# Output projections with 512-column matmuls, one weight tile at a time over all token blocks

## The chip, the cores and the metric

One core of one Trainium2 chip runs the whole program. The metric is device time in microseconds (us) of one execution; the kernel before takes 1948.97 us, the median of 3 runs that lie between 1947.54 and 1953.53 us.

## What is computed

A two-layer encoder step over 2048 prompt tokens and 8 samples of 16 tokens, d_model 1024, all in float32. Layer 0 joins banded attention and a gated delta rule, layer 1 takes trailing means. Each layer ends in an output projection of 1024 x 1024 that is added to the residual; these two products are what the change touches:

```python
def ab_layer(h, ...):
    ...
    y = h + jnp.concatenate([o_a, o_b], axis=-1) @ w_out
def pool_layer(h, ...):
    ...
    y = h + (mixed * jax.nn.silu(gate)) @ w_out
```

## The kernel before

Tokens are taken in four groups (`GROUPS`): group 0 has four prompt blocks and the one sample block of 128 tokens (nb = 5), groups 1 to 3 have four prompt blocks (nb = 4). For each group the program runs layer 0 and then layer 1. To keep float32 accuracy every product is three matmuls: operand and weight are each split into a rounded part and a rest (hi, lo), and hi x hi, hi x lo and lo x hi are summed in one PSUM bank.

**Weights** stream through a ring of three tiles (`wp`, tag "w", `NWB` = 3), hi and lo together 1 MB. In group 0 a tile is loaded from the input in float32 (`w_load`, L447), split by ACT (cast, L459) and by POOL and DVE (subtract, L463; `SHARE` says which rows of it POOL takes), and stored to a scratch copy `wk` (`w_store`, L472). In groups 1 to 3 it is loaded from `wk` (L436). `weight()` for tile n issues the load of tile n + 2, which must wait until tile n - 1 is no longer read. All DMAs are issued by one engine, SP, in program order.

**The output projection** is `out_half` (L713 to L732). It is called twice per layer, each time for half of the 1024 contraction rows (`ops0`, `ops1`: four operands of 128 rows each), so eight times in all. A weight tile holds four row blocks by 256 columns. For every tile the blocks of tokens are taken in turn; each block gets 12 matmuls of 256 columns in one PSUM bank of the tag "pj" (two banks), and then VectorE (DVE) adds the result to the residual `y1[b]` (L729). Where `done` is given (second half of a layer), the last two tiles are taken together, block by block, and after each block `done(b)` is called: in layer 0 it normalises the finished row block for layer 1 (`normed`: L514 to L534, later transposes L543), in layer 1 it issues the store of the output row block (L1774).

```python
for k, (oh, ol) in enumerate(ops):
    mm(pp[:, 0:256], oh[:, tk], wh[:, k, :], start=(k == 0), stop=False)
    mm(pp[:, 0:256], oh[:, tk], wl[:, k, :], start=False, stop=False)
    mm(pp[:, 0:256], ol[:, tk], wh[:, k, :], start=False, stop=(k == 3))
```

**Side work** runs in generators that are advanced by `tick(us)`, called between matmuls: the program's order is set by this assumed time, and a scheduler then fixes the order on each engine. During `out_half` of layer 1 the input of the next group is prepared (`norm_input`): two chunks of two blocks; of each, x is loaded (L508) and squared (L514, L516), POOL forms the inverse root (`rs`, L489), TensorE (PE) transposes it (L577), and L583 to L586 write the operand XH, XL. After the last `out_half` of a group comes `tok_major` of the next one (L1255 to L1257), which uses two weight tiles, the first for k < 4 and the second for k >= 4. PSUM has eight banks: two each for the tags "pj", "rc", "sc" and "tp". "rc" and "sc" serve the attention and delta-rule jobs, which are finished before `out_half` starts.

Of the kernel before, what the change touches and what calls it, by code (L numbers as in the profile page):

```python
# [10 lines left out]
ALU = mybir.AluOpType  # L11
# [4 lines left out]
P = 128  # L16
# [74 lines left out]
def weight_plan():  # L91

    import numpy as np

    plan = []

    def add(part, cut):
        plan.append((part, cut))

    def cols(name, c):  # L100
        return lambda w: w[name][:, c].reshape(KT, P, len(c)).transpose(1, 0, 2)

    def rows(name, k0, c0):
        return lambda w: w[name].reshape(KT, P, D)[k0:k0 + 4, :, c0:c0 + 256].transpose(1, 0, 2)

    def k_half(name, k0, c):
        return lambda w: w[name].reshape(KT, P, -1)[k0:k0 + 4][:, :, c].transpose(1, 0, 2)

    def out_rows(pr, c0):
        def cut(w):  # L110
            a = w["out"][0:512].reshape(2, 4, 64, D)[:, 2 * pr:2 * pr + 2, :, c0:c0 + 256]
            b = w["out"][512:].reshape(4, P, D)[2 * pr:2 * pr + 2, :, c0:c0 + 256]
            return np.concatenate([a.transpose(0, 2, 1, 3).reshape(P, 2, 256), b.transpose(1, 0, 2)], axis=1)
        return cut

    def grp(gi):
        return lambda w: w["grp"][gi].reshape(2, P, 256).transpose(1, 0, 2)

    def span(c0, n):
        return np.arange(c0, c0 + n)  # L120

    def keys(pr):
        for h in (2 * pr, 2 * pr + 1):
            add("B", cols("in", span(C_B + 512 + P * h, P)))

    def queries(pr):
        for o in (0, 1024):
            for h in (2 * pr, 2 * pr + 1):
                add("B", cols("in", span(C_B + o + P * h, P)))

    def queries_a(pr):
        c = np.concatenate([span(C_Q + 256 * g + P * pr, P) for g in range(2)])
        for k in range(2):
            add("A", k_half("in", 4 * k, c))

    for k in range(2):
        add("A", k_half("in", 4 * k, np.concatenate([span(C_K, 256), span(C_BA, 8)])))
    for pr in range(2):
        keys(pr)
        if pr == 0:  # L140
            queries_a(pr)
        queries(pr)
        if pr:
            queries_a(pr)
    for pr in range(2):
        for h in (2 * pr, 2 * pr + 1):
            add("G", cols("in", span(C_BG + P * h, P)))
        for j in (2 * pr, 2 * pr + 1):
            add("G", cols("in", np.concatenate([span(C_G + 256 * g + 64 * j, 64) for g in range(2)])))
    for pr in range(2):  # L150
        for c in range(4):
            add("O", out_rows(pr, 256 * c))
    for gi in range(4):
        for o in (0, D):
            for i in (2 * gi, 2 * gi + 1):
                add("C", cols("in_c", span(o + P * i, P)))
        add("W", grp(gi))
    for hf in range(2):
        for c in range(4):
            add("O", rows("out_c", 4 * hf, 256 * c))  # L160
    return plan

W_SHAPE = {"B": (8, P), "G": (8, P), "C": (8, P), "O": (4, 256), "W": (2, 256), "A": (4, 256)}
W_FIRST = (4, 264)

VECS = [("g_ab", KT), ("g_c", KT), ("scale", KT), ("o_norm", 1), ("q_norm", 1), ("taps", 48), ("k_norm", 64), ("k_col", 1),
# [63 lines left out]
def hybrid_kernel(  # L232
# [241 lines left out]
    def weight():  # L474
        n = wpos[0]
        wpos[0] += 1
        while wpos[1] <= min(n + 2, len(plan) - 1):
            w_load(wpos[1])
            wpos[1] += 1
        w_split(n + 1)  # L480

        w_store(1)
        if n + 1 == nw:
            w_store(0)
        return ready.pop(n)
# [180 lines left out]
    def group(gix, norm_job):  # L666
# [43 lines left out]
            drop(a)  # L710
            return [(h[:, i, 0:n], lo[:, i, 0:n]) for i in range(2)], [h, lo]

        def out_half(ops, y1, done=None):  # L713

            steps = [(0,), (1,), (2,), (3,)] if done is None else [(0,), (1,), (2, 3)]
            for cs in steps:
                ws = [weight() for _ in cs]
                for b in range(nb):
                    tk = slice(P * b, P * b + P)
                    for c, (wh, wl) in zip(cs, ws):  # L720
                        pp = psum("pj")
                        for k, (oh, ol) in enumerate(ops):
                            mm(pp[:, 0:256], oh[:, tk], wh[:, k, :], start=(k == 0), stop=False)  # L723
                            mm(pp[:, 0:256], oh[:, tk], wl[:, k, :], start=False, stop=False)  # L724
                            mm(pp[:, 0:256], ol[:, tk], wh[:, k, :], start=False, stop=(k == 3))  # L725
                            if k == 1:
                                tick(0.64)
                        ysl = y1[b][:, 256 * c:256 * c + 256]
                        V.tensor_tensor(ysl, pp[:, 0:256], ysl, op=ALU.add)  # L729
                        if done is not None and c == 3:  # L730
                            done(b)
                        tick(0.64)  # L732

        finish(norm_job)

# [909 lines left out]

                queue.append(cols())

        out_half(ops1, y1, normed)
        drop(*used1)
        drain()  # L1650

# [119 lines left out]
        out_half(ops0, y1)  # L1771
        drop(*used0)
        drain()
        out_half(ops1, y1, lambda b: Q.dma_start(rows(y, b), y1[b]))  # L1774
        drop(*used1)
        drop(*y1)

# [25 lines left out]
```

## Time and profile before

| | |
|---|---|
| median of 3 runs | 1948.97 us |
| profiled execution, its own time | 1951.19 us |
| its span | 1949.2 us, 34495 instructions |
| PE busy / weight loads (PEld) / DVE / ACT / POOL | 96% / 87% / 63% / 39% / 25% |
| DMA engines | 48.8% of their span for the one queue, 172 GB/s |

The span is that of the profiled execution; its own time is 2 us longer. Matmuls overlap in the pipe, so the durations of single matmuls add up to more than their busy time: how fast a stream of them runs is read from the distance of their starts. PE is the engine that is nearly always busy; idle time of the others costs nothing unless PE waits for it.

### The profile page before, as it was taken

Reading aid. Unit: us, or ns where it says so; the run is one execution under the profiler, and the core shown is the slowest. Engines: PE = TensorE matmul, PEld = TensorE weight load, DVE = VectorE, ACT = ScalarE, POOL = GpSimd, SP = SyncE. Lnnn points to the kernel's source line nnn. Section 1 sums busy time; section 2 is a strip of 40 time slices with the busy share of each in tenths; the row PEclk is TensorE's granted clock in tenths of the full one; section 3 lists DMA queues with packets and bytes.
Section 4 is the critical chain, followed back from the end, with each engine's and each line's share of the span. In section 5 each row is a group of like instructions: output and inputs, shape, how many; then the busy total and the mean of one; then the engine's idle time right before and its main releaser. Section 6 shows DMA issues by size and latency. Waiting matters only on the chain.

```text
span 1949.2 us, 34495 instructions
## 1 busy us (share of the span) xinstructions
PE 1863.0 (96%) x12994; PEld 1687.7 (87%) x12994; DVE 1218.5 (63%) x3439; ACT 758.5 (39%) x1954; POOL 496.2 (25%) x628
## 2 busy tenths in 40 slices
PE   5988989999999999899999999999999999999999
PEld 4988888899999888789889888789889978789889
DVE  5797967545665597764445597764345597764442
ACT  5465336333332474442221474442221474342210
POOL 3622451423343413210112413210111413110000
PEclk8998999999999999999999999999999999999999
DMA  7343363655677533434467533434567533434454
GB/s 261 96 161 133 109 217 101 221 190 212 211 264 263 200 115 118 151 120 173 178 218 261 176 114 115 151 121 172 188 218 263 183 114 101 158 115 173 172 193 176
DMA packets 93875, 335.13 MB, mean 172 GB/s; under 512 B 35805, under 2 KB 44253, under 8 KB 64269
## 3 DMA queue, kind: packets, MB, share of 16 engines
q1 hardware_dynamic: 93708, 332.92, 48.8%
q8 instruction: 103, 1.69, 0.3%
q14 instruction: 64, 0.52, 0.1%
HBM read 254.31 MB, written 78.58 MB: 171 GB/s over the span
## 4 chain that ended last, share of the span: by engine, by line
PE 76%; DVE 14%; issue 3%; DMA 2%; POOL 2%; ACT 2%; SPq 0%; DVEq 0%; POOLq 0%; ACTq 0%
PE pj L688 12%; PE pj L690 12%; PE pj L689 12%; PE pj L723 6%; PE pj L724 6%; PE pj L725 6%; DVE tm L969 3%; DVE A L970 2%; PE pj L1255 1%; PE pj L1257 1%; PE pj L1256 1%; PE tp L1434 1%; PE rc L1140 1%; DVE B L846 1%; DMA w<-wk 1%
## 5 line engine op out<-in xcount | busy, mean ns | idle before, releaser
L688 PE MATMUL pj<-XH,w 128*128 128x512 f32 (+3 forms) x1488 | 543.5, 365 | 5.4 <-ACT cb L826 3.3
L689 PE MATMUL pj<-XL,w 128*128 128x512 f32 (+3 forms) x1488 | 535.5, 360 | 0.0
L690 PE MATMUL pj<-XH,w 128*128 128x512 f32 (+3 forms) x1488 | 534.7, 359 | 0.3 <-POOL w L463 0.3
L688 PEld LDWEIGHTS pj<-XH,w 128*128 128x128 f32 x1488 | 283.9, 191 | 34.6 <-ACT cb L826 3.5
L690 PEld LDWEIGHTS pj<-XH,w 128*128 128x128 f32 x1488 | 283.6, 191 | 30.9 <-POOL w L463 0.6
L689 PEld LDWEIGHTS pj<-XL,w 128*128 128x128 f32 x1488 | 284.2, 191 | 27.7 <-issue 0.7
L725 PE MATMUL pj<-w,B 128*128 128x256 f32 x864 | 243.5, 282 | 0.0
L723 PE MATMUL pj<-w,B 128*128 128x256 f32 x768 | 217.8, 284 | 1.4 <-DVE A L729 1.4
L724 PE MATMUL pj<-w,B 128*128 128x256 f32 x768 | 217.3, 283 | 1.5 <-POOL w L463 1.5
L725 PEld LDWEIGHTS pj<-w,B 128*128 128x128 f32 x864 | 164.3, 190 | 0.0
L463 POOL TENSOR_TENSOR w<-wst,w 128x640 fp32r<-128x640 f32 (+3 forms) x60 | 112.1, 1870 | 145.2 <-ACT w L459 136.3
L723 PEld LDWEIGHTS pj<-w,B 128*128 128x128 f32 x768 | 146.5, 191 | 1.9 <-DVE A L729 1.6
L724 PEld LDWEIGHTS pj<-w,B 128*128 128x128 f32 x768 | 145.5, 189 | 1.7 <-POOL w L463 1.7
L729 DVE TENSOR_TENSOR B<-pj,B 128x256 f32<-128x256 f32 x144 | 60.8, 422 | 100.4 <-PE pj L725 99.5
L1255 PE MATMUL pj<-w,XH 128*128 128x256 f32 (+1 forms) x368 | 108.7, 296 | 5.2 <-DMA w<-wk 4.8
L1257 PE MATMUL pj<-w,XL 128*128 128x256 f32 (+1 forms) x368 | 106.1, 289 | 0.0
L1256 PE MATMUL pj<-w,XH 128*128 128x256 f32 (+1 forms) x368 | 105.8, 288 | 0.0
L729 DVE TENSOR_TENSOR A<-pj,A 128x256 f32<-128x256 f32 x128 | 54.0, 422 | 79.6 <-PE pj L725 79.3
L723 PE MATMUL pj<-w,A 128*128 128x256 f32 x320 | 91.5, 286 | 0.0
L724 PE MATMUL pj<-w,A 128*128 128x256 f32 x320 | 90.8, 284 | 0.0
L459 ACT CAST w<-wst 128x1024 fp32r<-128x1024 f32 (+1 forms) x60 | 61.2, 1019 | 58.0 <-PE pj L725 44.2
L701 DVE SCALAR_TENSOR_TENSOR A<-A,pj 128x512 f32<-128x512 f32 x36 | 24.7, 686 | 90.9 <-ACT A L700 90.9
(469 smaller groups left out, 4141.8 us busy)
## 6 DMA issues: line engine op xcount, KB each, us to landing
w<-wk SPq DMA_DIRECT2D x168, 1024.0 KB, 4.8
wk<-w SPq DMA_DIRECT2D x56, 1024.0 KB, 6.6
wst<-in_wts SPq DMA_DIRECT2D x56, 512.0 KB, 4.5
A<-in_x SPq DMA_DIRECT2D x22, 512.0 KB, 3.9
w<-wk SPq DMA_DIRECT2D x6, 1056.0 KB, 5.7
B<-in_x SPq DMA_DIRECT2D x12, 512.0 KB, 4.8
w<-wk SPq DMA_DIRECT2D x12, 512.0 KB, 3.3
out_y<-B SPq DMA_DIRECT2D x9, 512.0 KB, 2.7
```

What stands on the lines that cost most here:

```text
L459: S.copy(hi, st)
L463: eng.tensor_tensor(lo[:, a:b], st[:, a:b], f32(hi[:, a:b]), op=ALU.subtract)
L688: mm(pp[:, 0:w], wh[:, k, :], xh[:, k, t0:t1], start=(k == 0), stop=False)
L689: mm(pp[:, 0:w], wh[:, k, :], xl[:, k, t0:t1], start=False, stop=False)
L690: mm(pp[:, 0:w], wl[:, k, :], xh[:, k, t0:t1], start=False, stop=(k == KT - 1))
L723: mm(pp[:, 0:256], oh[:, tk], wh[:, k, :], start=(k == 0), stop=False)
L724: mm(pp[:, 0:256], oh[:, tk], wl[:, k, :], start=False, stop=False)
L725: mm(pp[:, 0:256], ol[:, tk], wh[:, k, :], start=False, stop=(k == 3))
L729: V.tensor_tensor(ysl, pp[:, 0:256], ysl, op=ALU.add)
L1255: mm(pp[:, 0:N], xh[:, k, tk], wh[:, k % 4, :], start=(k == 0), stop=False)
L1256: mm(pp[:, 0:N], xh[:, k, tk], wl[:, k % 4, :], start=False, stop=False)
L1257: mm(pp[:, 0:N], xl[:, k, tk], wh[:, k % 4, :], start=False, stop=(k == KT - 1))
```

## The change

`out_half` now uses tiles of two row blocks by 512 columns (same bytes). For each of two column halves c it takes the first tile (kk = 0) over all token blocks, leaving each block's PSUM bank open, then the second tile (kk = 1) over all blocks; after a block's second six matmuls DVE adds 512 columns to the residual. The open banks are of the tags pj, pj, rc, rc and, for a fifth block, sc. With `by_block` (layer 0's second half, and the last group's end) the second column half takes both tiles together, block by block. `done(b)` is called in the second column half. `tick(0.64)` is called after every three matmuls, that is as often per stage as before. The split of a tile between POOL and DVE in group 0 follows the new shape: 512 columns each instead of 768 and 256.

```diff
@@ -101,16 +101,17 @@
         return lambda w: w[name][:, c].reshape(KT, P, len(c)).transpose(1, 0, 2)
 
     def rows(name, k0, c0):
-        return lambda w: w[name].reshape(KT, P, D)[k0:k0 + 4, :, c0:c0 + 256].transpose(1, 0, 2)
+        return lambda w: w[name].reshape(KT, P, D)[k0:k0 + 2, :, c0:c0 + 512].transpose(1, 0, 2)
 
     def k_half(name, k0, c):
         return lambda w: w[name].reshape(KT, P, -1)[k0:k0 + 4][:, :, c].transpose(1, 0, 2)
 
-    def out_rows(pr, c0):
+    def out_rows(pr, kk, c0):
         def cut(w):
-            a = w["out"][0:512].reshape(2, 4, 64, D)[:, 2 * pr:2 * pr + 2, :, c0:c0 + 256]
-            b = w["out"][512:].reshape(4, P, D)[2 * pr:2 * pr + 2, :, c0:c0 + 256]
-            return np.concatenate([a.transpose(0, 2, 1, 3).reshape(P, 2, 256), b.transpose(1, 0, 2)], axis=1)
+            if kk:
+                return w["out"][512:].reshape(4, P, D)[2 * pr:2 * pr + 2, :, c0:c0 + 512].transpose(1, 0, 2)
+            a = w["out"][0:512].reshape(2, 4, 64, D)[:, 2 * pr:2 * pr + 2, :, c0:c0 + 512]
+            return a.transpose(0, 2, 1, 3).reshape(P, 2, 512)
         return cut
 
     def grp(gi):
@@ -148,21 +149,23 @@
         for j in (2 * pr, 2 * pr + 1):
             add("G", cols("in", np.concatenate([span(C_G + 256 * g + 64 * j, 64) for g in range(2)])))
     for pr in range(2):
-        for c in range(4):
-            add("O", out_rows(pr, 256 * c))
+        for c in range(2):
+            for kk in range(2):
+                add("O", out_rows(pr, kk, 512 * c))
     for gi in range(4):
         for o in (0, D):
             for i in (2 * gi, 2 * gi + 1):
                 add("C", cols("in_c", span(o + P * i, P)))
         add("W", grp(gi))
     for hf in range(2):
-        for c in range(4):
-            add("O", rows("out_c", 4 * hf, 256 * c))
+        for c in range(2):
+            for kk in range(2):
+                add("O", rows("out_c", 4 * hf + 2 * kk, 512 * c))
     return plan
 
 
 
-W_SHAPE = {"B": (8, P), "G": (8, P), "C": (8, P), "O": (4, 256), "W": (2, 256), "A": (4, 256)}
+W_SHAPE = {"B": (8, P), "G": (8, P), "C": (8, P), "O": (2, 512), "W": (2, 256), "A": (4, 256)}
 W_FIRST = (4, 264)
 
 VECS = [("g_ab", KT), ("g_c", KT), ("scale", KT), ("o_norm", 1), ("q_norm", 1), ("taps", 48), ("k_norm", 64), ("k_col", 1),
@@ -710,26 +713,38 @@
             drop(a)
             return [(h[:, i, 0:n], lo[:, i, 0:n]) for i in range(2)], [h, lo]
 
-        def out_half(ops, y1, done=None):
-
-            steps = [(0,), (1,), (2,), (3,)] if done is None else [(0,), (1,), (2, 3)]
-            for cs in steps:
-                ws = [weight() for _ in cs]
-                for b in range(nb):
-                    tk = slice(P * b, P * b + P)
-                    for c, (wh, wl) in zip(cs, ws):
-                        pp = psum("pj")
-                        for k, (oh, ol) in enumerate(ops):
-                            mm(pp[:, 0:256], oh[:, tk], wh[:, k, :], start=(k == 0), stop=False)
-                            mm(pp[:, 0:256], oh[:, tk], wl[:, k, :], start=False, stop=False)
-                            mm(pp[:, 0:256], ol[:, tk], wh[:, k, :], start=False, stop=(k == 3))
-                            if k == 1:
-                                tick(0.64)
-                        ysl = y1[b][:, 256 * c:256 * c + 256]
-                        V.tensor_tensor(ysl, pp[:, 0:256], ysl, op=ALU.add)
-                        if done is not None and c == 3:
+        def out_half(ops, y1, done=None, by_block=False):
+
+            def products(pp, b, kk, wt):
+                tk = slice(P * b, P * b + P)
+                for k in range(2):
+                    oh, ol = ops[2 * kk + k]
+                    mm(pp, oh[:, tk], wt[0][:, k, :], start=(kk == k == 0), stop=False)
+                    mm(pp, oh[:, tk], wt[1][:, k, :], start=False, stop=False)
+                    mm(pp, ol[:, tk], wt[0][:, k, :], start=False, stop=(kk == k == 1))
+                    tick(0.64)
+
+            for c in range(2):
+
+                if c and by_block:
+                    ws = [weight() for _ in range(2)]
+                    seq = [(b, kk, ws[kk]) for b in range(nb) for kk in range(2)]
+                else:
+                    seq = [(b, kk, None) for kk in range(2) for b in range(nb)]
+                open_ = {}
+                for b, kk, wt in seq:
+                    if wt is None:
+                        if b == 0:
+                            cur = weight()
+                        wt = cur
+                    if kk == 0:
+                        open_[b] = psum(("pj", "pj", "rc", "rc", "sc")[b])
+                    products(open_[b], b, kk, wt)
+                    if kk:
+                        ysl = y1[b][:, 512 * c:512 * c + 512]
+                        V.tensor_tensor(ysl, open_.pop(b), ysl, op=ALU.add)
+                        if done is not None and c:
                             done(b)
-                        tick(0.64)
 
         finish(norm_job)
 
@@ -1645,7 +1660,7 @@
 
                 queue.append(cols())
 
-        out_half(ops1, y1, normed)
+        out_half(ops1, y1, normed, True)
         drop(*used1)
         drain()
 
@@ -1771,7 +1786,7 @@
         out_half(ops0, y1)
         drop(*used0)
         drain()
-        out_half(ops1, y1, lambda b: Q.dma_start(rows(y, b), y1[b]))
+        out_half(ops1, y1, lambda b: Q.dma_start(rows(y, b), y1[b]), last)
         drop(*used1)
         drop(*y1)
 
```

The built program keeps every other PE instruction; the matmuls of `out_half` are 1632 of 512 columns where they were 3264 of 256. Three places where the order moves (lines of the changed program after the first hunks are 3, later 15 higher):

PE, first `out_half` of layer 1 in group 1, around the first transposes of the next group's `rs` (L577, now L580). `w` is a weight tile, A and B are operand buffers, and the first name is the PSUM bank. Before, 79 matmuls of the stage stand ahead:

```order
L723 MATMUL pj_11907<-w_11773,A_1953_11318 128x256
L724 MATMUL pj_11907<-w_11773,A_1953_11318 128x256
L725 MATMUL pj_11907<-w_11773,B_1954_11319 128x256
L723 MATMUL pj_11907<-w_11773,B_1975_11479 128x256
L577 MATMUL tp_11914<-first,rs_11884 128x128 x2
L724 MATMUL pj_11907<-w_11773,B_1975_11479 128x256
L725 MATMUL pj_11907<-w_11773,B_1976_11480 128x256
```

and now 45 wide ones:

```order
L724 MATMUL rc_11037<-w_10989,B_1920_10696 128x512
L722 MATMUL rc_11044<-w_10989,B_1919_10695 128x512
L723 MATMUL rc_11044<-w_10989,B_1919_10695 128x512
L724 MATMUL rc_11044<-w_10989,B_1920_10696 128x512
L580 MATMUL tp_11084<-first,rs_11068 128x128 x2
L722 MATMUL rc_11044<-w_10989,B_1919_10695 128x512
```

The transposes moved from the seventh turn of 12 narrow matmuls (third block, second tile) to the eighth turn of six wide ones (fourth block, second tile).

DVE at the same place: the additions to the residual (L729, now L745), the squares of x (L516, now L519; `t,ss`), and the two small operations that lead to `rs` (`ms`). Before:

```order
L729 TENSOR_TENSOR A_1834_10467<-pj_11793,A_1834_10467 128x256
L729 TENSOR_TENSOR B_1835_10469<-pj_11821,B_1835_10469 128x256
L729 TENSOR_TENSOR B_1836_10471<-pj_11835,B_1836_10471 128x256
L729 TENSOR_TENSOR B_1837_10473<-pj_11849,B_1837_10473 128x256
L729 TENSOR_TENSOR A_1834_10467<-pj_11865,A_1834_10467 128x256
L516 SCALAR_TENSOR_TENSOR t_11879,ss_11872<-A_2015_11802 128x512
L522 TENSOR_TENSOR ms_11881<-ss_11872 128x2
L729 TENSOR_TENSOR B_1835_10469<-pj_11893,B_1835_10469 128x256
L523 TENSOR_SCALAR ms_11881<-ms_11881 128x2
```

and now:

```order
L745 TENSOR_TENSOR A_1794_9907<-pj_11009,A_1794_9907 128x512
L519 SCALAR_TENSOR_TENSOR t_11063,ss_11056<-A_1959_11015 128x512
L745 TENSOR_TENSOR B_1795_9909<-pj_11030,B_1795_9909 128x512
L525 TENSOR_TENSOR ms_11065<-ss_11056 128x2
L519 SCALAR_TENSOR_TENSOR t_11230,ss_11227<-A_1985_11190 128x512
L526 TENSOR_SCALAR ms_11065<-ms_11065 128x2
```

One addition stands ahead of the squares that `ms` needs where five did; behind them an addition and one more squaring, of the second chunk, stand ahead of the last step of `ms`.

SP at the end of group 1: the last loads of the stage, the stores of the output and the two tiles of the next group's `tok_major` (wk_73 and wk_74). Before:

```order
L436 DMA w_12146<-wk_134 128x2048
L436 DMA w_12232<-wk_73 128x2112
L1774 DMA out_y<-A_1834_10467 128x1024
L1774 DMA out_y<-B_1835_10469 128x1024
L1774 DMA out_y<-B_1836_10471 128x1024
L436 DMA w_12234<-wk_74 128x2112
L1774 DMA out_y<-B_1837_10473 128x1024
L436 DMA w_12378<-wk_75 128x2048
```

and now:

```order
L439 DMA w_11222<-wk_134 128x2048
L439 DMA w_11280<-wk_73 128x2112
L439 DMA w_11325<-wk_74 128x2112
L1789 DMA out_y<-A_1794_9907 128x1024
L1789 DMA out_y<-B_1795_9909 128x1024
L1789 DMA out_y<-B_1796_9911 128x1024
L1789 DMA out_y<-B_1797_9913 128x1024
L439 DMA w_11370<-wk_75 128x2048
```

The load of the second tile moved ahead of all stores; the load after it still stands behind the last store.

## Rows read from the trace of the kernel before

**Rows 1.** page, busy time and clock: engines, and 40 slices of the span

```profile
PE 1863.0 (96%) x12994; PEld 1687.7 (87%) x12994; DVE 1218.5 (63%) x3439; ACT 758.5 (39%) x1954; POOL 496.2 (25%) x628
PEclk8998999999999999999999999999999999999999
```

**Rows 2.** page, chain that ended last, by line

```profile
PE pj L688 12%; PE pj L690 12%; PE pj L689 12%; PE pj L723 6%; PE pj L724 6%; PE pj L725 6%; DVE tm L969 3%; DVE A L970 2%; PE pj L1255 1%; PE pj L1257 1%; PE pj L1256 1%; PE tp L1434 1%; PE rc L1140 1%; DVE B L846 1%; DMA w<-wk 1%
```

**Rows 3.** page, groups: out_half matmuls and additions; count, busy us, mean ns, idle

```profile
L725 PE MATMUL pj<-w,B 128*128 128x256 f32 x864 | 243.5, 282 | 0.0
L729 DVE TENSOR_TENSOR B<-pj,B 128x256 f32<-128x256 f32 x144 | 60.8, 422 | 100.4 <-PE pj L725 99.5
L701 DVE SCALAR_TENSOR_TENSOR A<-A,pj 128x512 f32<-128x512 f32 x36 | 24.7, 686 | 90.9 <-ACT A L700 90.9
```

**Rows 4.** stretches, of the eight out_half stages: us, busy (x) of PE to POOL, PEclk, DMA, GB/s

```profile
573.00:634.00 61.00, 58.15 (x487) 57.42 (x486) 31.69 (x77) 14.64 (x28) 20.88 (x17) 1.00 0.78 280
1021.00:1069.00 48.00, 46.57 (x391) 46.14 (x390) 26.54 (x67) 10.28 (x26) 10.01 (x12) 1.00 0.73 267
1899.00:1945.00 46.00, 46.00 (x385) 45.92 (x385) 14.51 (x33) 1.22 (x2) 1.29 (x1) 1.00 0.50 189
sum 411.00, PE 403.31 PEld 399.74 DVE 197.57 ACT 83.19 POOL 74.30; mean PE 50.41 PEld 49.97 DVE 24.70 ACT 10.40 POOL 9.29
```

**Rows 5.** timeline of DVE, last stage: start us, us, line, [idle <-releaser]

```profile
1902.32 0.42 DVE L729 TENSOR_TENSOR B<-pj,B 128x256 f32<-128x256 f32 x1 [1.00 <-PE pj L725]
...
1920.87 0.42 DVE L729 TENSOR_TENSOR B<-pj,B 128x256 f32<-128x256 f32 x1 [1.00 <-PE pj L725]
...
1923.74 0.42 DVE L729 TENSOR_TENSOR A<-pj,A 128x256 f32<-128x256 f32 x1 [1.02 <-PE pj L725]
...
1945.33 0.42 DVE L729 TENSOR_TENSOR B<-pj,B 128x256 f32<-128x256 f32 x1 [1.01 <-PE pj L725]
```

**Rows 6.** timeline of PE, projection of layer 1, last group

```profile
1887.72 0.39 PE L688 MATMUL pj<-XH,w 128*128 128x512 f32 x1
...
1895.88 0.39 PE L688 MATMUL pj<-XH,w 128*128 128x512 f32 x1
```

**Rows 7.** waits of PE: us in total, times, longest us

```profile
PE tp L577 <- POOL rs L489: 10.4, 3, 8.1
PE pj L1255 <- DMA w<-wk: 4.8, 3, 2.1
PE tp L543 <- ACT A L533: 2.1, 4, 0.6
PE tp L543 <- DVE ms L523: 2.0, 1, 2.0
PE pj L724 <- POOL w L463: 1.5, 1, 1.5
PE pj L723 <- DVE A L729: 1.4, 1, 1.4
PE pj L1255 <- DVE A L729: 0.4, 1, 0.4
```

**Rows 8.** timeline of DVE, group 0, first out_half of layer 1

```profile
583.52 0.42 DVE L729 TENSOR_TENSOR A<-pj,A 128x256 f32<-128x256 f32 x1 [0.97 <-PE pj L725]
586.59 0.69 DVE L516 SCALAR_TENSOR_TENSOR t<-B 128x512 f32<-128x512 f32 x1 [2.65 <-DMA B<-in_x]
```

**Rows 9.** timeline of PE, group 1, first out_half of layer 1

```profile
1032.18 0.43 PE L577 MATMUL tp<-first,rs 128*128 128x128 f32 x2 [1.43 <-POOL rs L489]
```

**Rows 10.** timeline of PE, start of group 2

```profile
1074.15 0.54 PE L1255 MATMUL pj<-w,XH 128*128 128x264 f32 x1 [2.10 <-DMA w<-wk]
```

**Rows 11.** page, DMA issues: KB each, median us to landing

```profile
w<-wk SPq DMA_DIRECT2D x168, 1024.0 KB, 4.8
w<-wk SPq DMA_DIRECT2D x6, 1056.0 KB, 5.7
```

## Prediction

> **What bounds the kernel now.** I read the busy times first, then the chain, the stages, the starts of single matmuls, and last the waits of PE. PE is busy 96% of the span, and after the first slices the granted clock is 0.9 or more of the full 2.4 GHz [rows 1]. The chain that ended last runs through PE for most of its length; the three lines of the output projection hold 6% each [rows 2]. So what PE saves in these stages counts in full, unless it then waits for another engine. The eight stages of `out_half` last 411 us together in the stretches that I cut, and PE is busy for 403 us of them; the clock is 1.00 in each [rows 4]. DVE is busy for less than half of them, ACT and POOL for less. Their matmuls have a mean duration of 282 ns [rows 3], but they overlap: what counts is how far apart they start.
>
> **The rate, narrow against wide.** In the last stage PE never waits, and DVE's additions, one for every 12 narrow matmuls, give the pace. From 1902.32 to 1920.87 there are 13 such steps, 18.55 us, which is 1.427 us for 12 matmuls or 118.9 ns each; from 1923.74 to 1945.33 there are 15, 21.59 us, 119.9 ns each [rows 5]. I take 119.4. The projection of layer 1 already runs matmuls of 512 columns with the same types, a weight load ahead of each: 36 of them from 1887.72 to 1895.88, 226.7 ns each [rows 6]. Two narrow ones cost 238.8 ns, one wide one 226.7: 12.1 ns less. The change turns 3264 narrow ones into 1632 wide ones, so 1632 x 12.1 ns = **19.7 us** less. With 118.9 it would be 18.1, with 119.9 it would be 21.4; these are the bounds. The roles differ (here the tokens are loaded as weights and the weights stream, in the other projection the other way round), but both operands are 128-row SBUF tiles of one type, so I see no reason for another pace.
>
> The Trainium skill has a rule that speaks against so much (TensorE: Matmul & The Clock Gate, section "Wait — 56ns, not 53.3ns?"): warm matmuls start N / 2.4 GHz plus about 2.5 ns apart. An estimate by that page is 109.2 and 215.8 ns, 2.6 ns per pair, some 4 us in all. The rows disagree with it: they show some 12 and 13 ns above the columns' time, and the measurement decides.
>
> **Waits of PE that lie in these stages.** PE lost 1.4 us for a bank that DVE had not emptied [rows 7]: DVE stood still for 2.65 us, because the squares of x ahead of the addition waited for the load of x [rows 8]. With two banks PE reaches that wait after one block's turn; now a bank is asked for again four or five turns later, 5.4 us or more, and the stall of DVE is covered. Gain 1.4, and 0.4 for the same kind of wait at the start of `tok_major` [rows 7]. If that cover went, the cost is what it was. PE lost 1.5 us for the split of a weight in the last, paired sweep of group 0 [rows 7]; the sweep is no longer paired there, a tile is needed one sweep (6.8 us) after its predecessor, and POOL has 512 columns to do instead of 768. Gain 1.5.
>
> PE lost 4.8 us in three places at `tok_major` for its second weight tile [rows 7], 2.1 in one [rows 10]. In the paired sweep the buffer of that tile is free only one turn before the end; 12 narrow matmuls (1.43 us) and 12 more of `tok_major` are less than the 5.7 us that such a load takes to land [rows 11]. Now the next to last tile is done one sweep before the end, 24 x 226.7 ns = 5.44 us, and another 1.44 us pass before it is needed: 6.9 against 5.7. SP also issues it ahead of the stores, so it does not stand behind them. Gain 4.8. The load behind the last store starts later (the last addition, see below) but is needed only after all of `tok_major`, 96 matmuls or 11 us. Together 1.4 + 0.4 + 1.5 + 4.8 = **8.1 us**. The bounds are 0 (each comes back as another wait) and 8.1.
>
> **What becomes later.** First, `rs` for the next group. PE waits for it three times, 10.4 us; 8.1 of that is at the start, so 2.3 lie in groups 1 and 2 [rows 7], 1.43 in the one shown [rows 9]. PE now gets there after 45 x 226.7 = 10.2 us of the stage, before after 79 x 0.119 = 9.4. But DVE has the squares behind an addition that ends later, and one addition of some 0.69 us and one squaring of 0.69 [rows 8] between them and the last step of `ms`, where it had one of 0.42. So `rs` comes about 1 us later and PE 0.8 later: I take 0.25 each, 0.5 in all, bounds -2.3 and +3. Second, additions of 512 columns: no row shows that one. The nearest is another DVE operation of 128x512 out of PSUM, 686 ns against 422 for the 256 columns [rows 3]; I take 0.69, bounds 0.42 and 0.84. DVE does 136 of them instead of 272 and saves time, but the last one of a stage ends 0.27 us later. That lies on the path twice: at the end of the kernel ahead of the last store, and in group 0 ahead of the norm of the fifth block, for which PE already waits 2.0 us [rows 7]. That is 0.5. The four waits for the scaled rows (2.1 us [rows 7]) have the later addition against a PE that gets there later too; I leave them, bounds -2.1 and +1. Third, in group 0 the second chunk's transposes now stand 4 wide matmuls ahead of `tok_major`, where 36 narrow ones (4.3 us) stood before. The operand is needed two blocks later (48 x 0.12 = 5.8 us), about as long as eight pairs of DVE operations take; but ACT does the casts and also empties the banks of `tok_major`. I take 1.0, bounds 0 and 3.
>
> Nothing for: ticks, which come as often per stage; DMA bytes, the same; weight supply, since a tile needs 4.8 us to land [rows 11] and is asked for two sweeps (10.9 us) ahead; the order of the other engines in the other stages, which the built program leaves as it was.
>
> **The sum.** -19.7 - 8.1 + 0.5 + 0.5 + 1.0 = -25.8. The profiled execution took 1951.19 us by itself, so 1925.4; it lies 2.2 us above the median of the runs. I say **1925**.
>
> **Rivals.** *The waits come back* (chance 0.13). PE is faster by 5% in these stages while the DMAs are not, and DMA is busy 0.73 to 0.78 of the first stages of layer 1 [rows 4]; a wait that ends with a landing only moves. For it: the squares that held DVE waited for a load, not for an engine [rows 8]. Against it: the deeper banks. Then only the rate is left and the later steps cost 3 us in all: 1951.2 - 19.7 + 3 = 1934.5.
>
> *Wide matmuls pace no better here* (0.04). If the 12 ns went with columns and not with instructions in this place, the rate's term is 0: 1951.2 - 8.1 + 2.0 = 1945.1. Against it stand rows 6. The skill's rule above would be a milder form of this, about 1941 by the page.
>
> *Weights come late* (0.03), the one on the other side. Each sweep now takes 5.44 us for 1 MB, and the ring of three lets a load start only when the tile three before it is done. If a load took more than two sweeps, 10.9 us, every one of the 32 sweeps would wait for the rest. At 12.5 us that is 32 x 1.6 = 51 us, 1951.2 - 25.8 + 51 = 1977; it is slower than before from 11.7 us on. For it: at 267 to 280 GB/s the stages of layer 1 are the heaviest for DMA after the start [rows 4], and the stores of the output, 2 MB, now leave within one sweep. Against it: loads land in 4.8 us [rows 11], and PE never waited for a weight inside a stage of groups 1 to 3.
>
> *The change does not do what it says* would need the wide matmuls to be missing; they stand in the built program. No chance is set aside.
>
> **How the numbers follow.** The forecast has 0.80. Its own range: the rate between 18.1 and 21.4, the waits between 4 and 8.1, the later steps between -2 and 5, gives 1951 - 31.5 to 1951 - 17, 1920 to 1934. The run that is measured may lie 2 to 3 us lower, as the median of before does. The range of 1917 to 1938 takes in the first rival as well and leaves out the two others and part of the tails. 0.3% is 5.8 us, about what a measurement of this kernel can tell from no change: the bound is 1943. The forecast and the first rival are faster by more, the second lies about at the bound: faster 0.93, same 0.04, slower 0.03.
>
> **What would show it.** Starts of the 512-column matmuls of `out_half` 227 ns apart; the last stage 192 x 0.2267 = 43.5 us from its first to its last matmul, where 384 x 0.1194 = 45.8 stood; no wait of L1255's successor for a weight; no wait of PE for the addition or for POOL's split in `out_half`; the wait for `rs` still 2 to 3 us in groups 1 and 2. I am wrong if the pace there is 235 ns or more, or if PE's waits for a DMA, for `rs` or for XH grow by more than 5 us together.

## The result, and the profile after

| | before | after |
|---|---|---|
| median (range), 4 runs each, same chip | 1948.95 us (1947.54 to 1953.53) | 1927.64 us (1926.80 to 1928.33) |
| profiled execution, its own time | 1951.19 us | 1927.47 us |
| span | 1949.2 us | 1925.6 us |

The ratio is 0.9878, 95% interval 0.9864 to 0.9893: 1.2% faster (the two medians of the table by themselves give 0.9891). The forecast was 1925, and 25.8 us off the profiled execution; it became 23.7. Its terms missed by more than their sum did, in opposite directions.

The page of the changed kernel: busy times (answer to [rows 1]), the additions and one of the out_half groups ([rows 3]), and the loads of weights ([rows 11]). DVE issues 136 additions fewer, PE 1632 matmuls fewer.

```profile
PE 1843.6 (96%) x11362; PEld 1598.0 (83%) x11362; DVE 1208.0 (63%) x3303; ACT 759.2 (39%) x1954; POOL 494.1 (26%) x628
...
L745 DVE TENSOR_TENSOR A<-pj,A 128x512 f32<-128x512 f32 x40 | 27.6, 690 | 107.2 <-PE pj L724 107.2
...
L724 PE MATMUL rc<-w,B 128*128 128x512 f32 x200 | 79.0, 395 | 0.0
...
w<-wk SPq DMA_DIRECT2D x168, 1024.0 KB, 4.9
```

Three words that are used below: a stage is the output projection of one layer in one group, that is two calls of `out_half` (so there are eight stages and 16 calls in all, of four weight tiles each; the eight named further up is the count of the stages); a turn is one block of tokens with one weight tile; a sweep is one tile over all blocks.

The eight stages, each cut exactly from its first matmul's start to its last one's (the cuts of [rows 4] were a little wider, so before is cut again here). The columns are those of [rows 4]. First before, the sum alone:

```profile
sum 408.68, PE 400.99 PEld 397.80 DVE 197.37 ACT 82.84 POOL 74.09; mean PE 50.12 PEld 49.73 DVE 24.67 ACT 10.36 POOL 9.26
```

Then after, the stages of [rows 4] and the sum:

```profile
573.46:631.54 58.08, 56.47 (x252) 45.99 (x250) 26.71 (x52) 13.72 (x24) 17.94 (x16) 1.00 0.84 299
...
1015.93:1060.93 45.00, 44.77 (x197) 36.13 (x195) 25.52 (x51) 9.99 (x26) 10.18 (x13) 1.00 0.74 275
...
1877.39:1921.06 43.67, 43.67 (x193) 35.87 (x191) 11.73 (x17) 0.95 (x2) 1.29 (x1) 1.00 0.50 191
sum 391.42, PE 385.98 PEld 313.40 DVE 178.82 ACT 79.89 POOL 71.30; mean PE 48.25 PEld 39.17 DVE 22.35 ACT 9.99 POOL 8.91
```

The stages are 17.3 us shorter: PE is busy for 15.0 us less, and idle for 5.4 us instead of 7.7.

The waits of PE after (answer to [rows 7]). The wait of the key projection (`tok_major`) for its weight (L1255, now L1270), that for POOL's split and that for the addition are gone; what is left at L1270 that [rows 7] did not have is 0.3 us.

```profile
PE tp L580 <- POOL rs L492: 10.3, 4, 8.1
PE tp L546 <- DVE XL L548: 8.6, 12, 1.4
PE pj L1270 <- ACT XH L588: 3.2, 1, 3.2
PE tp L546 <- ACT A L536: 2.3, 4, 0.7
PE tp L546 <- DVE ms L526: 1.1, 1, 1.1
PE pj L1270 <- DVE VL L1316: 0.3, 1, 0.3
```

The waits for `rs` have the same sum as before, but they lie elsewhere. In groups 1 and 2 they fell from 1.43 and 0.91 us to 0.23 and 0.28. In group 0 there is a new one, 1.61 us, for the second chunk; before, the same transposes started at 629.78, 4.3 us ahead of the stage's last matmul, and did not wait:

```profile
630.57 0.43 PE L580 MATMUL tp<-first,rs 128*128 128x128 f32 x2 [1.61 <-POOL rs L492]
```

Where the 23.6 us of the span came from, then: the stages 17.3; the key projections of groups 1 to 3, from the last matmul of `out_half` to the last of `tok_major`, 8.6 (40.67, 42.74 and 42.55 us before, 39.51, 38.90 and 38.97 after, by the starts in the traces); given back 0.4 behind the last matmul and 1.7 before the first stage (1.5 when the same kernel ran again), where this case doesn't show why. The rest, 0.2 us given back, lies between the stages.

The last stage shows that the pace is not the same everywhere. These are starts of its first matmul and of every 24th one behind it, one sweep of four blocks each:

```profile
1877.39 0.39 PE L722 MATMUL pj<-w,A 128*128 128x512 f32 x1
...
1882.83 0.40 PE L722 MATMUL pj<-w,B 128*128 128x512 f32 x1
...
1888.42 0.39 PE L722 MATMUL pj<-w,A 128*128 128x512 f32 x1
...
1893.89 0.40 PE L722 MATMUL pj<-w,B 128*128 128x512 f32 x1
```

The sweeps take 5.44, 5.59 and 5.47 us: 226.7 ns, then 232.9, then 227.9 per matmul. The second loads its tokens from other slots than the first and third.

### The profile page after: what moved, and what is told of

It is laid out like the page before. It is cut to its first block, busy times and chain, and to the rows that moved or that the text cites. A ratio compares the mean times of both kernels' runs of the same rounds, so it can differ in the third digit from the quotient of the medians.

```text
span 1925.6 us, 31047 instructions
## 1 busy us (share of the span) xinstructions
PE 1843.6 (96%) x11362; PEld 1598.0 (83%) x11362; DVE 1208.0 (63%) x3303; ACT 759.2 (39%) x1954; POOL 494.1 (26%) x628
## 4 chain that ended last, share of the span: by engine, by line
PE 64%; DVE 9%; issue 2%; ACT 1%; POOL 1%; DMA 0%; SPq 0%; DVEq 0%; ACTq 0%; POOLq 0%
PE pj L691 11%; PE pj L693 11%; PE pj L692 11%; PE pj L724 2%; PE pj L722 2%; PE pj L723 2%; PE rc L724 2%; PE rc L722 2%; PE rc L723 2%; DVE tm L984 2%; PE pj L1270 1%; PE pj L1272 1%; PE pj L1271 1%; DVE A L985 1%; PE tp L1449 1%
## 5 line engine op out<-in xcount | busy, mean ns | idle before, releaser
L466 POOL TENSOR_TENSOR w<-wst,w 128x640 fp32r<-128x640 f32 (+2 forms) x60 | 106.6, 1778 | 152.3 <-ACT w L462 140.0
L1270 PE MATMUL pj<-w,XH 128*128 128x256 f32 (+1 forms) x368 | 106.7, 290 | 0.3 <-DVE VL L1316 0.3
L745 DVE TENSOR_TENSOR A<-pj,A 128x512 f32<-128x512 f32 x40 | 27.6, 690 | 107.2 <-PE pj L724 107.2
L724 PE MATMUL rc<-w,B 128*128 128x512 f32 x200 | 79.0, 395 | 0.0
L724 PE MATMUL pj<-w,B 128*128 128x512 f32 x200 | 78.6, 393 | 0.0
L466 DVE TENSOR_TENSOR w<-wst,w 128x384 fp32r<-128x384 f32 (+2 forms) x60 | 52.0, 866 | 33.5 <-ACT w L462 33.0
L1270 PEld LDWEIGHTS pj<-w,XH 128*128 128x128 f32 x368 | 69.9, 190 | 1.8 <-DVE VL L1316 0.6
L1271 PEld LDWEIGHTS pj<-w,XH 128*128 128x128 f32 x368 | 70.0, 190 | 1.1 <-issue 0.5
L722 PE MATMUL rc<-w,B 128*128 128x512 f32 x176 | 70.3, 399 | 0.0
L1272 PEld LDWEIGHTS pj<-w,XL 128*128 128x128 f32 x368 | 69.9, 190 | 0.0
L722 PE MATMUL pj<-w,B 128*128 128x512 f32 x176 | 69.4, 394 | 0.0
L723 PE MATMUL pj<-w,B 128*128 128x512 f32 x176 | 69.1, 393 | 0.0
```

What stands on the lines that cost most here:

```text
L466: eng.tensor_tensor(lo[:, a:b], st[:, a:b], f32(hi[:, a:b]), op=ALU.subtract)
L722: mm(pp, oh[:, tk], wt[0][:, k, :], start=(kk == k == 0), stop=False)
L723: mm(pp, oh[:, tk], wt[1][:, k, :], start=False, stop=False)
L724: mm(pp, ol[:, tk], wt[0][:, k, :], start=False, stop=(kk == k == 1))
L1270: mm(pp[:, 0:N], xh[:, k, tk], wh[:, k % 4, :], start=(k == 0), stop=False)
L1271: mm(pp[:, 0:N], xh[:, k, tk], wl[:, k % 4, :], start=False, stop=False)
```

## Experiments

Theory: the pace of the wide matmuls gives most, and the order by tiles gives the waits. Rival: the pace is worth little and the gain is the waits. A second question came with the profile after: why are some sweeps slower? The runs were taken on several chips, with the kernel before beside them on each; its median there was 1948.95 to 1953.60 us. So two kernels that ran on different chips are compared by their ratios to it and by their traces, and a difference of 2 us between their times tells nothing.

### The pace alone

e1_narrow_sweeps keeps sweeps and open banks, and splits 11 of the 12 wide matmuls of each bank:

```diff
-                    mm(pp, oh[:, tk], wt[0][:, k, :], start=(kk == k == 0), stop=False)
...
+                        for q in range(2):
+                            h = slice(256 * q, 256 * q + 256)
+                            mm(pp[:, h], o[:, tk], wt[i][:, k, h], start=False,
+                               stop=(kk == k == q == 1 and o is ol))
```

Expected: 

> The changed kernel with its sweeps and open banks, but 22 of the 24 matmuls of every bank 256 columns wide again (the one that opens a bank stays 512 wide). Theory 1, most of the gain is the pace: two narrow matmuls start 238.8 to 242 ns apart (before: 118.9 to 121), one wide one took 227 to 233 in the profile after; 136 banks x 11 pairs x 9 to 12 ns = 13 to 18 us slower than the changed kernel, so 1941 to 1946 us, with the waits at the start of the key projection (L1270 in the profile after) still gone. Theory 2, the gain is the waits that the sweeps and open banks removed, and the pace is worth little: within 3 us of the changed kernel, 1925 to 1931 us.

Measured: 1941.73 us (1940.09 to 1944.06), 0.9950 of before (0.9931 to 0.9969); 14 us over the changed kernel. Its eight stages, cut in the same way:

```profile
sum 408.26, PE 399.81 PEld 391.76 DVE 182.37 ACT 82.63 POOL 72.17; mean PE 49.98 PEld 48.97 DVE 22.80 ACT 10.33 POOL 9.02
```

The stages are as long as before the change, and PE is busy in them for 13.8 us more than with wide matmuls. Theory 1 holds: 1496 pairs at 9.2 ns. What e1 still gains over before, some 9.5 us, is what the order by tiles gives, and it lies outside the stages: its key projections in groups 1 to 3 are 9.4 us shorter than before.

### The order alone

e2_wide_paired keeps the width and takes both tiles of every column half together, block by block, with the banks of one ring:

```diff
-                if c and by_block:
+                if True:
...
-                        open_[b] = psum(("pj", "pj", "rc", "rc", "sc")[b])
+                        open_[b] = psum("pj")
```

Expected: 

> The changed kernel's 512-column matmuls, but both weight tiles of a column half taken together, block by block, with the two banks of one ring, in every stage: the sweeps and the open banks undone, the pace kept. Theory 1, the sweeps are worth the waits alone: PE waits again for a weight at the start of the key projection of groups 1 to 3 (4.8 us in three places before), for POOL's split (1.5) and for a bank (1.4): 5 to 10 us slower than the changed kernel, 1933 to 1938 us, still 10 us or more under the kernel before. Theory 2, the waits had moved anyway or hide behind something else: within 3 us of the changed kernel, 1925 to 1931 us. Theory 3, without the sweeps PE also waits for weights inside the stages (two tiles needed at once instead of one every 5.4 us): 1940 us or more.

Measured: 1964.39 us (1963.59 to 1966.27), 1.0068 of before (1.0048 to 1.0089). Theory 3, and worse than it said: 37 us over the changed kernel, slower than before. The edit undoes the open banks too, but the waits for a bank inside the stages are only 1.4 us of this. Waits of PE:

```profile
PE pj L722 <- DMA w<-wk: 15.9, 20, 1.4
...
PE pj L1270 <- DMA w<-wk: 5.3, 3, 2.6
...
PE pj L722 <- DVE A L745: 1.4, 3, 0.6
```

A column half needs two tiles at its first block and frees both in its last turn; of the ring of three only one tile is ahead, and the next pair's second tile lands too late, 20 times inside the stages. So the width alone, in an order that holds two tiles, loses more than it gives. (Before, only the last halves held two tiles, and these were the last two narrow quarters.)

e8_last_half_paired does this only where before did it, in the last half of layer 1 of the groups with a key projection behind them:

```diff
-        out_half(ops1, y1, lambda b: Q.dma_start(rows(y, b), y1[b]), last)
+        out_half(ops1, y1, lambda b: Q.dma_start(rows(y, b), y1[b]), True)
```

Expected: 

> The changed kernel, but with both weight tiles of the last column half taken together, block by block, at the end of layer 1 in the three groups that a key projection follows too; before the change the last two quarters were taken so. Theory 1 (the prediction's term): the buffer of the second tile of the key projection is free only one turn before the end again, and PE waits for that tile, 4.8 us in the sum of the prediction, up to 7.6 by what the transitions into groups 1 to 3 became shorter: 1932 to 1935 us, with a DMA wait at L1270. Theory 2, the loads that were late before were late for another reason (what stood ahead of them in SP's queue): no wait there, 1926 to 1929 us. It costs more than 10 us if the half itself, with two tiles needed at once, waits for its weights as in e2_wide_paired: about 1940 us.

Measured: 1935.30 us (1932.16 to 1938.22), 0.9913 of before (0.9898 to 0.9929); 7.7 us over the changed kernel (6.8 by the ratios). The stages have the lengths of the changed kernel; the wait is back:

```profile
PE pj L1270 <- DMA w<-wk: 5.9, 3, 2.6
```

Theory 1, 0.3 us above its upper end. The time lost is more than the wait: in the profiled execution the three key projections are 9.1 us longer than in the changed kernel. So it was before. Here is PE in the kernel before, behind its wait into group 2 [rows 10]:

```profile
1074.93 0.43 PE L1255 MATMUL pj<-w,XH 128*128 128x264 f32 x1
1075.15 0.42 PE L1256 MATMUL pj<-w,XH 128*128 128x264 f32 x1
...
1077.57 0.30 PE L1255 MATMUL pj<-w,XH 128*128 128x264 f32 x1
1077.71 0.28 PE L1256 MATMUL pj<-w,XH 128*128 128x264 f32 x1
1077.83 0.29 PE L1257 MATMUL pj<-w,XL 128*128 128x264 f32 x1
```

and the granted clock in that place (the last three columns are PEclk, DMA share, GB/s), before:

```profile
1068.90:1074.20 5.30, 3.20 (x27) 3.02 (x26) 0.42 (x1) 0.00 (x0) 0.57 (x2) 1.00 0.96 318
1074.20:1080.00 5.80, 5.80 (x35) 5.80 (x36) 1.21 (x6) 1.42 (x8) 1.38 (x3) 0.71 0.41 171
```

after:

```profile
1061.00:1066.00 5.00, 5.00 (x42) 4.96 (x41) 1.35 (x4) 0.71 (x4) 0.41 (x1) 1.00 1.01 392
1066.00:1072.00 6.00, 6.00 (x52) 6.00 (x51) 1.40 (x6) 1.68 (x9) 3.12 (x7) 1.00 0.41 153
```

and in e8_last_half_paired:

```profile
1068.00:1074.00 6.00, 5.99 (x37) 6.00 (x38) 1.45 (x6) 1.42 (x8) 1.50 (x3) 0.73 0.36 153
```

Behind 2.10 us of idle PE started a matmul every 0.22 us up to 1077.57, and every 0.12 us from there: for the first 15 of them the clock stood at its lower level, 1.2 of 2.4 GHz, which makes the mean of 0.71. They lost 0.1 us each, some 1.6 us on top of a wait of 2.1. The key projections into groups 2 and 3 became 3.84 and 3.58 us shorter, while the waits in them were 2.10 and 1.89. Not every such wait has this price, as the last section shows.

### Why some sweeps are slower

In the built program all streaming weight tiles start at 32 modulo 128 bytes of a partition, the token slots A0 to B6 too, B7 to B10 at 96. e3_slots_one_line moves these four by 64 bytes:

```diff
+        if gix == 0:
+            G.memset(buf([P, 16], "pad", 1), 0.0)
```

Expected: 

> The changed kernel plus one tile of 64 bytes per partition (a memset at the start of group 0) that shifts the addresses of four operand slots, so that all of them stand at 32 modulo 128 bytes instead of nine or more at 32 and four (B7 to B10) at 96. In the profile after, 512-column matmuls whose loaded operand lies in a slot at 32 start 226.7 ns apart and those at 96 some 231 to 233. Theory 1, the address modulo 128 sets this: all run at 226.7, the spread over 1632 matmuls goes, 5 to 7 us less than the changed kernel, 1921 to 1923 us. Theory 2, it is the region (the four slots are the last ones) or the turn of the stage, not the address modulo 128: the same slots stay at 231 to 233 ns and the time stays within 1.5 us of the changed kernel.

e4_all_at_0 adds `G.memset(const([P, 24], "pad0"), 0.0)` ahead of `XH`. Expected: 

> As e3_slots_one_line, with 96 bytes more per partition ahead of the operand slots, so that all of them stand at 0 modulo 128. Theory 1 (address modulo 128 sets the pace, 32 good and 96 bad): a start at 0 is either as good as 32, 226.7 ns and 1921 to 1923 us, or better, nearer to 512 columns at the full clock (213.3 ns), which over 1632 wide matmuls would be up to 20 us less. Theory 2 (region): the slots B7 to B10 stay at 231 to 233 ns and the time within 1.5 us of the changed kernel. If 0 is worse than 32: slower than e3_slots_one_line by what 4 to 6 ns over 1632 matmuls make, 6 to 10 us.

Measured: 1926.23 us (1925.07 to 1928.00) and 1925.81 (1925.30 to 1927.53). Theory 1 failed: sweeps that load from B7 became fast, those from B8 to B10 stayed at 231 to 233 ns. Theory 2 failed as well, since B7 changed by 64 bytes without leaving its place. But in all three kernels a sweep was fast where loaded and streaming operand had the same address modulo 256 (the weight tiles stand at 32 modulo 256 there, in e4 at 128). The next three test that; a table in `slot` adds the pads, here that of e5_same_mod_256:

```diff
+    PADS = {"B7": 16, "B8": 32}
...
+        if tag in PADS:
+            G.memset(buf([P, PADS.pop(tag)], "pad" + tag, 1), 0.0)
```

e6_slots_128_off has `"A0": 32` in it too; e7_all_128_off is e5 with 128 bytes ahead of `XH`.

Expected of e5: 

> The changed kernel with two pads (64 and 128 bytes per partition) so that the tokens' slots that are loaded (A0 to A5, B0 to B10) and the weight tiles that stream all stand at 32 modulo 256 bytes. In the profiles of the changed kernel, of e3_slots_one_line and of e4_all_at_0 the 512-column matmuls started 226.7 ns apart where both operands had the same address modulo 256, and 231 to 233 next to a loaded operand that had another. Theory 1, the difference modulo 256 of the two operands sets the pace: all sweeps at 226.7 to 228 now, where the mean of the 1632 was 229.9 in the changed kernel; 2 to 3 ns x 1632 = 3 to 5 us less, 1922 to 1925 us. Theory 2, the last three slots are slow by their place in the memory (from some 191 KB on): they stay at 231 to 233 and the time is that of e3_slots_one_line, 1925 to 1928 us.

Of e6: 

> As e5_same_mod_256, but every loaded slot 128 bytes further (160 modulo 256) while the weight tiles stay at 32. Theory 1 (difference modulo 256): all sweeps at about 233 ns, 1632 x 6 ns = 10 us more than e5_same_mod_256, 1932 to 1935 us. Theory 2 (place in the memory): the slots A0 to B7 stay at 226.7, B8 to B10 at 231 to 233, 1925 to 1928 us. Theory 3 (the loaded operand's own address modulo 256, whatever the streaming one's): as theory 1 here; the next run tells them apart. Other stages that load from these slots may move too; the stages of the output projection are what counts.

Of e7: 

> As e5_same_mod_256, with everything 128 bytes further: loaded slots and weight tiles both at 160 modulo 256. Theory 1 (difference of the two): as e5_same_mod_256, 226.7 to 228 ns, within 1.5 us of it. Theory 3 (the loaded operand's own address modulo 256): 233 ns as in e6_slots_128_off, 8 to 10 us more than e5_same_mod_256. Theory 2 (place in the memory): only B8 to B10 at 231 to 233, 1925 to 1928 us.

Measured: e5 1923.09 us (1921.49 to 1925.24), 0.9851 of before (0.9834 to 0.9869); e6 1932.07 (1931.29 to 1932.30), 0.9896 (0.9879 to 0.9913); e7 1921.87 (1920.97 to 1923.15), 0.9845 (0.9828 to 0.9862). Theory 1 holds, and the others fall: e6 against e5 shows the difference, e7 against e6 that the slot's own address does not matter. A larger modulus adds nothing: in e5 the distance is 226.9 ns where the starts agree modulo 512 too, and 227.1 where they agree only modulo 256. The last stage of e5, starts as above, 5.44 us a sweep:

```profile
1872.63 0.39 PE L725 MATMUL pj<-w,A 128*128 128x512 f32 x1
...
1878.07 0.39 PE L725 MATMUL pj<-w,B 128*128 128x512 f32 x1
...
1883.51 0.39 PE L725 MATMUL pj<-w,A 128*128 128x512 f32 x1
...
1888.95 0.39 PE L725 MATMUL pj<-w,B 128*128 128x512 f32 x1
```

and of e6, 5.60 us:

```profile
1880.62 0.40 PE L725 MATMUL pj<-w,A 128*128 128x512 f32 x1
...
1886.22 0.40 PE L725 MATMUL pj<-w,B 128*128 128x512 f32 x1
```

Mean distance of starts in all stages, by turn and by the address difference modulo 256 of its slots from the weight tile. Left out are matmuls next to an idle time, and the first distance behind a transpose, which is some 83 ns longer at either width (202 ns before, 313 after):

| kernel | all slots at 0 | some off | all off | mean |
|---|---|---|---|---|
| after, 512 wide | 227.9 ns (152 turns) | 232.0 (86) | 233.2 (34) | 229.8 |
| e3 | 227.3 (168) | 232.5 (88) | 232.8 (16) | 229.3 |
| e5 | 227.2 (272) | | | 227.2 |
| e6 | | | 232.8 (272) | 232.8 |
| e7 | 227.1 (272) | | | 227.1 |
| before, 256 wide | 120.2 (48) | 118.6 (224) | | 118.9 |
| e9 | 120.0 (272) | | | 120.0 |
| e10 | | | 119.3 (272) | 119.3 |

The expectations of e9 and e10 below have 121.4 and 120.2 ns for the kernel before; these figures take in the distances behind transposes.

Does it pay without the change? e9_before_same and e10_before_128_off are the kernel before with the pads of e5 and of e6; after_again is the changed kernel beside them.

Expected of e9: 

> The kernel before with the two pads of e5_same_mod_256: loaded slots and streaming weight tiles all at 32 modulo 256. In the profile before, 256-column matmuls started on the mean 121.4 ns apart where all operands had the same address modulo 256 and 118.5 to 120.4 elsewhere, 120.2 over all. Theory 1, narrow matmuls gain nothing from equal addresses: 120 to 121.5 ns, within 4 us of the kernel before, so the difference between narrow and wide is 2 x 120.7 - 227.2 = 14 ns per pair at equal addresses. Theory 2, equal addresses help narrow ones as they help wide ones (2.6 ns per wide one on the mean): 118.9 ns, 4 us less than before, and the pads are worth as much without the change.

Of e10: 

> The kernel before with the pads of e6_slots_128_off: every loaded slot 128 bytes off the weight tiles modulo 256, which cost the wide kernel 9 us against equal addresses. Theory 1 (narrow matmuls do not mind): 118.5 to 120.4 ns, from 0 to 5 us less than the kernel before. Theory 2 (they mind as the wide ones do, one load per matmul, 5.5 ns each): 3264 x 5 ns = 16 us more.

Of after_again: 

> The changed kernel as it is, beside the next two on one chip: 1926 to 1929 us, a mean pace of some 229.8 ns in its 512-column matmuls.

Measured: e9 1952.19 us (1948.99 to 1957.81), 1.0000 of before (0.9989 to 1.0012); e10 1950.78 (1948.60 to 1952.22), 0.9997 (0.9988 to 1.0005); after_again 1927.08 (1925.53 to 1927.67), 0.9874 (0.9859 to 0.9888). Theory 1 of both: narrow matmuls gain nothing from equal starts. If anything they lose: the stages of e9 last 3.0 us longer than those of before. So the 4 to 6 us that e5 and e7 gain over the changed kernel are there only with the width. The times of these two lie below those of both kernels, and their ranges do not meet those of the changed kernel. That comparison is across chips, and the interval of e5's ratio overlaps that of the changed kernel; what the traces show is the stages, 387.6 and 387.7 us against 391.4.

## Why the prediction was right, and where it was not

**The rate** (19.7 us): right in kind, too large, and outside its bounds of 18.1 to 21.4. PE's busy time in the stages fell by 15.0 us. The step that was mis-sized is the pace: 226.7 ns was read from a projection whose two operands, by the built program, both start at 32 modulo 256 [rows 6], and taken for all 1632 matmuls, with no reason seen for another pace. In 120 of 272 turns of `out_half` a slot stood off the weight tile, and the mean was 229.8. Narrow ones were a little faster than the 119.4 of the last stage, 118.9 on the mean. So a pair gave 8.0 ns instead of 12.1, 13.1 us. Another 1.0 us came from fewer first matmuls behind a transpose or a wait, 30 where there were 42; 0.9 us stays open. With equal addresses, in e5, the busy time falls 19.3 us below that of before, nearly the term as forecast:

```profile
sum 387.62, PE 381.68 PEld 313.26 DVE 178.62 ACT 79.93 POOL 69.84; mean PE 47.71 PEld 39.16 DVE 22.33 ACT 9.99 POOL 8.73
```

That the rate carries most is shown by e1. By the rule of the Trainium skill on the distance of warm matmuls (TensorE: Matmul & The Clock Gate, section "Wait — 56ns, not 53.3ns?") an estimate would be 2.6 ns for a pair. The traces disagree: 8.0 ns by the table, and e1 lost 9.2.

**The waits in the stages** (1.4 for a bank, 1.5 for the split, 0.5 given back at `rs` and 1.0 for the second chunk of group 0: 1.4): idle time there fell by 2.3. The first two are gone as worked out. In groups 1 and 2 the step on `rs` had the wrong sign: `rs` came as early in the stage as before (10.7 us behind its start in group 1, where it was 11.0), PE got there later as forecast, and the wait fell by 1.8 instead of growing by 0.5. The second chunk cost 1.6, within its bounds of 0 to 3, as the wait for `rs` at 630.57; the wait for its operand XH is 3.2 us where it was 3.4. Waits in the first stage grew by 0.65, which no term had.

**The key projection** (4.8 and 0.4: 5.2): 8.6. The waits are gone as worked out, 1.25 us in group 0, 2.10 and 1.89 in the two others, and e8 brings them back. What the step left out is the clock behind a wait: 1.7 us each time into groups 2 and 3 of this execution. The Trainium skill (TensorE: Matmul & The Clock Gate, section "What's actually happening") has the slow state as the default and activity as what lifts it. The rows at 0.71 and 0.73 agree: the clock fell behind idle time and came back while PE was working. But this price was not certain, so 3.4 of the 8.6 us are luck: in e9, whose waits are nearly those of before (1.95 and 1.69 us), the clock stayed at 1.00 and the same two key projections took 41.07 and 40.82 us instead of 42.74 and 42.55.

**The tail**: 0.4 of the 0.5 set down for two places, with additions of 0.69 us as taken from [rows 3]; the other place, the norm of the fifth block, had a shorter wait (`ms`, 2.0 us before, 1.1 after).

**The rivals.** The waits did not come back, because a tile is asked for in time; e2 shows that this is the order's doing and not the width's. Wide matmuls did pace better, by 8.0 ns a pair. "Weights come late" was worked out with loads that take longer, and with 32 sweeps; the stages have 64 tiles, 48 of them in groups 1 to 3, so its price of 51 us was too low. It needs no such loads: in e2, with two tiles held, PE waited for them 20 times inside the stages, and the kernel was slower than before. It did not happen here because one tile is held at a time in most of the sweeps.

So the mechanism was right and the total was nearly right by luck: 4.7 us too much for the rate, against 3.4 too little for the key projections and 0.9 too little for the waits; the 1.7 us lost ahead of the first stage were in no term.

## What to carry to other kernels

Widening a matmul pays per instruction, but it must come with an order that asks for its tiles in time: here the change was worth 21 us with one tile held, 14 of them by the width (e1), and the same width with two tiles held cost 13 (e2 against before). A wait of PE costs more than its idle time where the clock falls behind it, as it did behind six of ten such waits here; look at the stretch behind the wait and not only at the row of the wait. Before a pace is taken from another stage, compare where the operands lie: for 512-column f32 matmuls an equal start modulo 256 bytes was worth 2.5% of the pace, for the price of a pad.

## What the hardware showed that was not expected

The distance of 512-column matmuls depends on the start of the loaded operand against the streaming one modulo 256 bytes: 227.2 ns on the mean at 0 (e5), 232.8 at 128 (e6), 233.2 at 64 and 192 and 232.0 where only some of a turn's loads are off (the changed kernel). At 256 columns it went the other way, and by less: 120.0 at 0 (e9), 119.3 at 128 (e10), and in the kernel before 118.6 where some of a turn's loads are off by 64 or 192. Why this is so was not found.

In the kernel before the clock fell behind the waits of 2.10 and 1.89 us in the key projection, and stayed at 1.00 behind the two of 0.45 and 0.81 us in that of group 0. These are the stretches behind the second of those in group 0, and behind the wait of 1.89 us:

```profile
640.00:644.00 4.00, 4.00 (x35) 4.00 (x34) 1.32 (x6) 1.42 (x8) 1.96 (x4) 1.00 0.46 182
...
1510.80:1516.80 6.00, 5.97 (x36) 6.00 (x37) 1.32 (x6) 1.42 (x8) 1.50 (x3) 0.72 0.44 182
```

The length of the wait does not decide it. Behind the longest waits of the key projection in e2 and in e9, 2.61 and 1.95 us, the clock stayed at 1.00; here is each wait with the stretch behind it, first e2, then e9:

```profile
1080.34 0.36 PE L1270 MATMUL pj<-w,XH 128*128 128x264 f32 x1 [2.61 <-DMA w<-wk]
1080.00:1086.00 6.00, 5.67 (x47) 5.70 (x48) 1.32 (x6) 1.42 (x8) 2.38 (x5) 1.00 0.42 175
...
1075.45 0.36 PE L1258 MATMUL pj<-w,XH 128*128 128x264 f32 x1 [1.95 <-DMA w<-wk]
1075.60:1081.40 5.80, 5.80 (x49) 5.80 (x50) 1.33 (x6) 1.43 (x8) 2.59 (x6) 1.00 0.39 162
```

Over the key projections into groups 2 and 3 of before, e2, e8, e9 and e10, the clock fell to 0.71 to 0.73 behind six of ten waits of 1.69 to 2.64 us. What decides it was not found.

In the stages of e2 it stayed at 1.00 too, with 20 waits of up to 1.4 us each; here is one of the stages, with four of them:

```profile
1465.40:1516.50 51.10, 46.11 (x196) 35.70 (x195) 25.69 (x51) 10.14 (x26) 11.28 (x13) 1.00 0.67 245
```
